# Grouped-query attention: three score blocks on VectorE in two jobs of three, and the checks and loads rearranged

## The chip, the core and the metric

The kernel runs on one core of a Trainium2 chip. The engines named here are TensorE (PE in the profile; PEld is its weight load), VectorE (DVE), ScalarE (ACT), GpSimd (POOL) and SyncE (SP, which here only issues DMAs). The metric is the device time of one execution in microseconds (us), as the median of several runs. Beside these, one execution was profiled; the trace and all durations come from that one.

## The reference

Grouped-query attention in float32: 8 batches, sequences of 512, 32 query heads, 8 key/value heads, head size 64. Four query heads share one key/value head.

```python
scale = 1.0 / np.sqrt(dim)
K_expanded = np.repeat(K, heads_per_group, axis=2)
V_expanded = np.repeat(V, heads_per_group, axis=2)
...
scores = np.einsum('bhqd,bhkd->bhqk', Q, K_expanded) * scale
weights = np.exp(scores - np.max(scores, axis=-1, keepdims=True))
weights = weights / (np.sum(weights, axis=-1, keepdims=True) + 1e-10)
output = np.einsum('bhqk,bhkd->bhqd', weights, V_expanded)
```

## The kernel before

**Jobs.** The work is cut into 64 jobs. Job j belongs to unit u = j // 2 and is one key/value head with its four query heads, in two pairs (i = 0, 1). Four units make a batch, so a batch is eight jobs. The scores of a job are 16 blocks of 128 keys x 512 queries: pair i, key chunk kc (four chunks of 128), head m within the pair. `scores` (L257) computes one block on TensorE with the keys as weights; the two heads of a pair lie in the two halves of the 128 rows.

**Exponentials.** Most blocks go through ScalarE: `act_tile` (L273) has TensorE write two blocks into a tile `s_ps` and ScalarE write their exponential into `pt` (L279). The pool of `s_ps` holds two tiles, so TensorE may be two tiles ahead. Some blocks of the second pair go through VectorE and GpSimd instead. `taken(j)` (L242) says how many: two in a narrow job, three in a wide one (`WIDE`, L41: every even job from 4 on). Their scores go to a tile `d_ps` (a pool of one tile with two banks of 512 columns), and then:

- `exp_d` (L283): VectorE turns them into 16-bit integers u (L290), two blocks in one instruction, the third block in one of its own;
- `exp_d2` (L297): VectorE takes the low bits f of u with an AND (L301), GpSimd computes g from f (L304) and w = g * f (L308);
- `exp_d4` (L314): VectorE adds u and w into `pt` (L317). This happens one job later; the text calls it the add.

In a wide job the fourth of seven ScalarE tiles, counted from 0, holds one block alone. It has no `s_ps` tile: its scores go into the second bank of the `d_ps` tile in whose first bank Q is transposed (L559 to L565), and ScalarE reads them there ("the half tile").

**Products.** `pv` (L333) multiplies the exponentials with V, to which a column of ones is appended, so that sums come out beside the products; 64 small matmuls a job, for the job before (`last`), in pieces between the score tiles (`cut`, L539, says where the second pair's are split). `norm` (L372) takes the reciprocal of the sums (L387) and multiplies into `o_sb` (L392) on VectorE. The pool of `pv` holds one tile, so the next 32 products wait for L392 of the 32 before. `store` writes a unit out through SP.

**Checks.** The exponentials need no maximum as long as sums stay within bounds and V is not huge. `check_sums` (L363) tests 16 pairs' reciprocals at a time with two VectorE operations (L356); `check_v` (L230) takes the largest absolute value of a quarter of a batch's V (L232). A slower general path runs behind a branch if a test fails; with these inputs it does not.

**Transposes and loads.** Q is loaded in its natural layout with a cast to bf16 (`load_q`, L132, GpSimd's queue), transposed by TensorE two jobs ahead (L210), and copied by VectorE into `qt` (L214). K is loaded the same way (`load_k`, L111) and transposed by DMA on SP's queue (`dma_k`, L185). V goes into one of two buffers (`load_v`, L120).

**Order.** The order of the program is the order in which each engine works: the code is issued under a manual schedule, nothing is rearranged, and every engine takes its instructions one after the other. The loop over jobs is L518 to L582. Where two instructions touch different banks of one tile, `apart` declares that they need not wait for each other; every other shared tile makes them wait. The third block of the next job is written into the second bank of the tile `bank` of this job, behind tile 5:

```python
act_tile(j, 5)
if taken(j + 1) > 2:
    exp_d(j + 1, 2, taken(j + 1), bank[:, 1:2, :], copies[0])()
pv(last, 1, *cut)
act_tile(j, 6)
pv(last, 1, cut[1], 32)
norm(last, 1)
```

Of the kernel before, what the change touches and what calls it, by code (L numbers as in the profile page):

```python
# [12 lines left out]
FP32 = mybir.dt.float32  # L13
BF16 = mybir.dt.bfloat16
# [4 lines left out]
ALU = mybir.AluOpType  # L19
EXP = mybir.ActivationFunctionType.Exp  # L20
COPY = mybir.ActivationFunctionType.Copy
AX = mybir.AxisListType
# [15 lines left out]
LAST_SUMS = NLAST * 2 * 4  # L38


WIDE = lambda j: j >= 4 and j % 2 == 0  # L41


@with_exitstack
# [23 lines left out]
def fast_path(ctx, tc, Q, K, V, out, flag, ident):  # L68
    nc = tc.nc
    B, S, H, D = Q.shape  # L70
    KV = K.shape[2]
    HPG = H // KV
    SC = S // 128
    GP = KV // 2
    NU = B * GP
# [6 lines left out]
    const_pool = ctx.enter_context(tc.tile_pool(name="const", bufs=1))  # L82
    qnat_pool = ctx.enter_context(tc.tile_pool(name="qnat", bufs=4))
# [11 lines left out]
    pv_pool = ctx.enter_context(tc.tile_pool(name="pv", bufs=1, space=PS))  # L95

    ok = const_pool.tile([128, SPB * 2 * SC], FP32, name="ok")
    okv = const_pool.tile([128, B * SC], FP32, name="okv")
    okall = const_pool.tile([128, 1], FP32, name="okall")
    gate = const_pool.tile([1, 1], FP16, name="gate")  # L100
    warm = const_pool.tile([128, S], BF16, name="warm")
# [2 lines left out]
    vt = [const_pool.tile([128, SC, KV, D + 1], BF16, name=f"v{j}") for j in range(2)]  # L104
# [4 lines left out]
    kn, qn, kt, qt, twice = {}, {}, {}, {}, {}  # L109

    def load_k(b, lo=0, hi=KV):  # L111
        if b not in kn:
            kn[b] = knat_pool.tile([128, SC, KV, D], BF16, name="k_nat")
        nc.gpsimd.dma_start(
            out=kn[b][:, :, lo:hi, :],
            in_=K[b, :, lo:hi, :].rearrange("(sc p) g d -> p sc g d", p=128),
        )


    def load_v(b, lo=0, hi=KV, chunks=range(SC)):  # L120
        for sc in chunks:
            nc.gpsimd.dma_start(  # L122
                out=vt[b % 2][:, sc, lo:hi, 0:D],
                in_=V[b, sc * 128:(sc + 1) * 128, lo:hi, :],
            )

    def load_v_head(b, g):
        nc.gpsimd.dma_start(
            out=vt[b % 2][:, :, g, 0:D], in_=V[b, :, g, :].rearrange("(sc p) d -> p sc d", p=128)
        )  # L130

    def load_q(u, lo=0, hi=2 * HPG):  # L132
        b, gp = divmod(u, GP)
        h0 = gp * 2 * HPG
        if u not in qn:
            qn[u] = qnat_pool.tile([128, SC, 2 * HPG, D], BF16, name="q_nat")
        nc.gpsimd.dma_start(  # L137
            out=qn[u][:, :, lo:hi, :],
            in_=Q[b, :, h0 + lo:h0 + hi, :].rearrange("(sc p) h d -> p sc h d", p=128),
        )  # L140

# [60 lines left out]
    def trans_q(j, bank, lo=0, hi=NPAIR, other=None):  # L202
        u, g = divmod(j, 2)
        ps = bank.bitcast(BF16).rearrange("p (i sc c) -> p i sc c", i=NPAIR, sc=SC)
        done = []
        for i in range(lo, hi):
            for sc in range(SC):
                h = g * HPG + 2 * i
                done.append(apart(
                    nc.tensor.transpose(ps[:, i, sc, :], qn[u][:, sc, h:h + 2, :], ident), other  # L210
                ))
        if u not in qt:
            qt[u] = qt_pool.tile([128, 2, NPAIR, S], BF16, name="qt")
        return done, lambda: apart(nc.vector.tensor_copy(  # L214
            out=qt[u][:, g, lo:hi, :], in_=ps[:, lo:hi, :, :].rearrange("p i sc c -> p i (sc c)")
        ), other)
# [10 lines left out]
                    apart(copy, before)  # L227
        pieces.append((bank, done, copy))

    def check_v(b, sc):  # L230
        n = b * SC + sc
        nc.vector.tensor_reduce(  # L232
            out=okv[:, n:n + 1], in_=vt[b % 2][:, sc, :, 0:D], op=ALU.max, axis=AX.XY,
            apply_absolute_value=True,
        )

    NJOB = NU * 2
    DPAIR = NPAIR - 1  # L240
# [1 line left out]
    def taken(j):  # L242
        return 1 if j == NJOB - 1 else 3 if WIDE(j) else 2

# [8 lines left out]
        return [[every[n] for n in group] for group in groups if group]  # L253

    jobs, osb, invs = {}, {}, {}

    def scores(j, ps, i, kc, m):  # L257
        u, g = divmod(j, 2)
# [38 lines left out]
    def exp_d2(j, engine=None):  # L297
        st = jobs[j]
        by_bits = engine is None
        engine = engine or nc.gpsimd  # L300
        nc.vector.tensor_single_scalar(  # L301
            out=st["f"], in_=st["u"], scalar=1023, op=ALU.bitwise_and
        )
        engine.tensor_scalar(  # L304
            out=st["g"], in0=st["f"], scalar1=-EXP_F1, scalar2=EXP_K * 2.0 ** (24 * by_bits),
            op0=ALU.add, op1=ALU.mult,
        )
        product = lambda: engine.tensor_tensor(  # L308
            out=st["w"], in0=st["g"], in1=st["f"].bitcast(FP16) if by_bits else st["f"],
            op=ALU.mult,  # L310
        )
        return product() if by_bits else product

    def exp_d4(j):  # L314
        st = jobs[j]
        n = taken(j)
        nc.vector.tensor_tensor(  # L317
            out=st["pt"][:, DPAIR, :, :, :].rearrange("p kc m q -> p (kc m) q")[
                :, d_block(j):d_block(j) + n, :
            ].bitcast(U16),  # L320
            in0=st["u"],
            in1=st["w"],
            op=ALU.add,
        )
# [38 lines left out]
    def check_sums():  # L363
        while full:
            k, n = full.pop()
            cols = n * 2 * SC
            flat = invs.pop(k).rearrange("p s m qc -> p (s m qc)")[:, 0:cols]
            in_bounds((ok[:, 0:cols], ok[:, 0:cols]), flat, ok[:, 0:cols])
# [79 lines left out]
        return s_pool.tile([128, 2, S], FP32, name="s_ps")  # L448

    def key_head(g, queue):  # L450
        queue.dma_start(out=kf[g], in_=K[0, :, g, :].rearrange("(sc p) d -> p sc d", p=128))

    key_head(0, nc.sync)
    nc.scalar.dma_start(out=qf, in_=Q[0, :, 0:2, :].rearrange("(sc p) h d -> p sc h d", p=128))
# [5 lines left out]
    for j in range(2):  # L460
        nc.gpsimd.memset(vt[j][:, :, :, D:D + 1], 1.0)
    load_k(0, 2, 4)
    load_q(1)
    load_v_head(0, 1)
    load_k(0, 4, KV)
    load_v(0, 2, KV)
    nc.gpsimd.memset(ones, 1.0)
    nc.gpsimd.memset(ok, 1.0)

# [48 lines left out]
    for j in range(1, NJOB - 1):  # L518
        last = j - 1
        u, g = divmod(j, 2)  # L520
        b, gp = divmod(u, GP)
        open_job(j)
        if j == 1:

            nc.gpsimd.tensor_copy(out=gate, in_=jobs[0]["pt"][0:1, 0, SC - 1, 0, 0:1])
            load_q(2)
            load_q(3)
        if g == 0 and u >= 1 and u + 3 < NU:
            load_q(u + 3)
        if (gp, g) == (1, 0) and b + 1 < B:  # L530
            load_k(b + 1)
        if 3 <= 2 * gp + g < 3 + SC and b + 1 < B:
            load_v(b + 1, chunks=(2 * gp + g - 3,))
        if j == 1:
            dma_k(0, 2)
        if gp == 2 and g == 0 and b + 1 < B:
            dma_k(b + 1)

        cut = (4, 18) if taken(j) > 2 else (11, 19)  # L539
        act_tile(j, 0)  # L540
        if j == 1:
            piece(1, *first_k(1, 0, bank[:, 1, S // 2:]))
        exp_d(j, 0, 2, d_tile())()
        act_tile(j, 1)

        if j == 8:
            check_v(0, 0)
        if g == 1 and 1 < j and b < B - 1:
            check_v(b, gp)
        if 0 <= j - 8 * (B - 1) < SC:  # L550
            check_v(B - 1, j - 8 * (B - 1))
        pv(last, 0, 0, 16)
        act_tile(j, 2)
        pv(last, 0, 16, 32)
        norm(last, 0)
        act_tile(j, 3)

        reads = []
        bank = d_tile()  # L559
        beside = act_tile(j, 4, bank) if taken(j) > 2 else None  # L560

        ahead = (j + 1,) if j < 2 else (3, 4) if j == 2 else (j + 2,)
        for n, to in enumerate(ahead):
            if to < NJOB:
                reads.append(trans_q(to, bank[:, n, :], other=beside)[1])  # L565
        if j == 1:
            reads.append(first_k(1, 1, bank[:, 1, :])[1])
        exp_d4(last)
        check_sums()
        exp_d2(j)  # L570
        copies = [read() for read in reads]
        if taken(j) == 2:
            act_tile(j, 4)
        pv(last, 1, 0, cut[0])
# [7 lines that stand above are left out]
        del jobs[last]  # L582
# [146 lines left out]
```

## Time and profile before

| | |
|---|---|
| median of 3 runs | 411.63 us (411.63 to 411.84) |
| the profiled execution | 412.08 us |
| its span, first to last instruction | 410.3 us |
| busy: ScalarE | 401.0 us (98% of the span), 454 instructions |
| busy: TensorE | 377.9 us (92%) |
| busy: VectorE | 342.3 us (83%) |
| busy: GpSimd | 305.9 us (75%) |
| waiting longest: GpSimd's g for VectorE's f | 90.9 us in 62 waits |
| granted TensorE clock | 0.999 |

How to read the lines below. A timeline line gives the start, the duration, the engine, the line of the kernel, the operation, and what it writes and reads; "x16" merges 16 like instructions in a row, and then the duration runs from the first start to the last end. A line of groups gives the number of instructions behind the x, then their busy time in us and the mean duration of one in ns, and behind the next bar the idle time of the engine just ahead of them and what ended it. A line of waits reads: who waited for whom, us in total, how many times, the longest. Instructions of one engine overlap: one starts while the one before it drains, so durations add up to more than the busy time. In the stretch that is used most, the job that starts at 198.99 us is narrow (j = 31) and the one that starts at 205.41 us is wide (j = 32).

### The profile page before, as it was taken

How to read it: one execution, taken by the hardware profiler on the slowest of the kernel's cores; microseconds unless marked ns; L12 is line 12 of the kernel's file. 1: busy time of each engine (PE TensorE's matmuls, PEld its weight loads, DVE VectorE, ACT ScalarE, POOL GpSimd, SP SyncE). 2: the span in 40 equal slices, each digit the busy share in tenths (PEclk: the TensorE clock that was granted, in tenths of full speed). 3: DMA queues.
4: the chain of work that ended last, by engine and by line, in shares of the span. 5: the costliest groups of instructions: out<-in, count | busy, mean ns of one | idle time of the engine just before them, and what ended most of it. 6: DMA issues, size and time to landing. Idle time of an engine off the chain costs nothing.

```text
span 410.3 us, 13045 instructions
## 1 busy us (share of the span) xinstructions
PE 377.9 (92%) x5666; PEld 233.0 (57%) x5666; DVE 342.3 (83%) x608; ACT 401.0 (98%) x454; POOL 305.9 (75%) x216
## 2 busy tenths in 40 slices
PE   7999999999999999999999999999999999999985
PEld 3565565555555655655555655655655555655543
DVE  4787898888898888888888888888889888998775
ACT  5999999999999999999999999999999999999995
POOL 9858767888678777688777897587786887676562
PEclk9999999999999999999999999999999999999999
DMA  9999974999839995499995999669996799752206
GB/s 142 167 242 166 201 158 138 188 148 214 170 109 227 126 263 127 113 211 107 203 255 83 205 188 215 157 84 215 183 191 155 132 205 204 145 144 104 104 18 195
DMA packets 93278, 67.74 MB, mean 165 GB/s; under 512 B 53280, under 2 KB 76320, under 8 KB 93216
## 3 DMA queue, kind: packets, MB, share of 16 engines
q0 software_dynamic: 55488, 24.91, 54.6%
q1 hardware_dynamic: 36672, 41.56, 36.6%
q8 instruction: 45, 0.74, 0.8%
q10 hardware_dynamic: 1056, 0.39, 0.4%
q14 instruction: 17, 0.14, 0.1%
HBM read 50.33 MB, written 33.55 MB: 204 GB/s over the span
## 4 chain that ended last, share of the span: by engine, by line
ACT 88%; PE 8%; DVE 2%; issue 1%; ACTq 0%; DVEq 0%
ACT pt L279 88%; PE s_ps L261 5%; PE pv L345 2%; PE s_ps L473 1%; DVE o_sb L392 1%; DVE pt L317 0%; ACTq L279 0%; DVE inv_last L387 0%; DVE qt L214 0%; PE pv L490 0%; PE d_ps L345 0%; DVE u L290 0%; ACT qt L495 0%; PE d_ps L261 0%; DVE ok L356 0%
## 5 line engine op out<-in xcount | busy, mean ns | idle before, releaser
L279 ACT ACTIVATE pt<-s_ps 128x1024 f16<-128x1024 f32 x419 | 396.3, 1295 | 0.7 <-PE s_ps L261 0.7
L345 PEld LDWEIGHTS <-pt 128*128 128x128 f16 x4096 | 142.3, 98 | 75.7 <-issue 55.3
L345 PE MATMUL pv<-v,pt 128*128 128x65 bf16 x4064 | 179.4, 195 | 0.9 <-DVE o_sb L392 0.7
L261 PE MATMUL s_ps<-qt,kt 64*128 64x512 bf16 x781 | 153.3, 383 | 23.3 <-ACT pt L279 17.1
L308 POOL TENSOR_TENSOR w<-g,f 128x1024 bf16<-128x1024 bf16 (+1 forms) x63 | 162.9, 2586 | 5.2
L304 POOL TENSOR_SCALAR g<-f 128x1024 bf16<-128x1024 int16 (+1 forms) x63 | 78.3, 1242 | 91.0 <-DVE f L301 90.9
L290 DVE TENSOR_SCALAR u<-d_ps 128x1024 int16<-128x1024 f32 (+1 forms) x94 | 97.6, 1038 | 0.5 <-PE d_ps L261 0.5
L261 PEld LDWEIGHTS <-kt 64*128 64x128 bf16 x960 | 55.3, 93 | 66.2 <-issue 37.0
L392 DVE TENSOR_TENSOR o_sb<-pv,inv 128x512 f32<-128x512 f32 x121 | 83.7, 692 | 4.2
L387 DVE RECIPROCAL inv<-pv 128x8 f32<-128x8 f32 x121 | 25.1, 207 | 49.7 <-PE pv L345 49.7
L317 DVE TENSOR_TENSOR pt<-u,w 128x1536 uint16<-128x1536 int16 (+1 forms) x64 | 51.4, 803 | 0.3 <-POOL w L308 0.2
L261 PE MATMUL d_ps<-qt,kt 64*128 64x512 bf16 x179 | 46.1, 375 | 0.1
L214 DVE COPY qt<-d_ps 128x1024 bf16<-128x1024 bf16 x62 | 42.3, 683 | 0.0
L210 PEld LDWEIGHTS <-q_nat 128*128 128x128 bf16 x508 | 28.5, 98 | 20.2 <-issue 20.2
L210 PE MATMUL d_ps<-ident,q_nat 128*128 128x128 bf16 x496 | 38.3, 221 | 0.0
L301 DVE TENSOR_SCALAR f<-u 128x1536 int16<-128x1536 int16 (+1 forms) x64 | 30.7, 480 | 0.0
L122 POOL DMA_DIRECT2D v<-in_V_dram x32 | 29.0, 914 | 0.0
L137 POOL DMA_DIRECT2D q_nat<-in_Q_dram x33 | 27.0, 820 | 0.1
L279 ACT ACTIVATE pt<-d_ps 128x512 f16<-128x512 f32 x30 | 26.7, 889 | 0.0
L232 DVE TENSOR_REDUCE okv<-v 128x1 f32<-128x512 bf16 x32 | 21.6, 675 | 0.0
L261 PE MATMUL s_ps<-qt,kt_first 64*128 64x512 bf16 x56 | 11.2, 390 | 2.1 <-ACT pt L279 1.7
L261 PEld LDWEIGHTS <-kt_first 64*128 64x128 bf16 x64 | 4.1, 93 | 6.0 <-issue 3.5
(54 smaller groups left out, 46.8 us busy)
## 6 DMA issues: line engine op xcount, KB each, us to landing
out_dram<-o_sb SPq DMA_DIRECT2D x31, 1024.0 KB, 7.2
q_nat<-in_Q_dram POOLq DMA_DIRECT2D x31, 512.0 KB, 6.1
k_nat<-in_K_dram POOLq DMA_DIRECT2D x7, 512.0 KB, 8.7
v<-in_V_dram POOLq DMA_DIRECT2D x28, 128.0 KB, 7.2
kt<-kt SPq DMA_DIRECT2D x14, 256.0 KB, 4.1
out_dram<-o_sb SPq DMA_DIRECT2D x4, 256.0 KB, 2.2
kt<-k_nat SPq DMA_TRANSPOSE x32, 5.9
v<-in_V_dram POOLq DMA_DIRECT2D x4, 96.0 KB, 8.3
```

Of the source, the lines that this page charges most:

```text
L122: nc.gpsimd.dma_start(out=vt[b % 2][:, sc, lo:hi, 0:D], in_=V[b, sc * 128:(sc + 1) * 128, lo:hi, :],)
L210: nc.tensor.transpose(ps[:, i, sc, :], qn[u][:, sc, h:h + 2, :], ident), other
L214: return done, lambda: apart(nc.vector.tensor_copy(out=qt[u][:, g, lo:hi, :], in_=ps[:, lo:hi, :, :].rearrange("p i sc c -> p i (sc c)")), ...
L261: return nc.tensor.matmul(ps, keys[64 * m:64 * m + 64, g if u == 0 else g ^ m, kc * 128:(kc + 1) * 128], qt[u][64 * m:64 * m + 64, g, i, : ...
L279: return nc.scalar.activation(out=jobs[j]["pt"][:, i, kc, lo:, :], in_=ps[:, lo:, :], func=EXP, scale=scale)
L290: return lambda: nc.vector.tensor_scalar(out=st["u"][:, lo:hi, :], in0=ps[:, 0:hi - lo, :], scalar1=A_U, scalar2=B_U, op0=ALU.mult, op1=AL ...
L301: nc.vector.tensor_single_scalar(out=st["f"], in_=st["u"], scalar=1023, op=ALU.bitwise_and)
L304: engine.tensor_scalar(out=st["g"], in0=st["f"], scalar1=-EXP_F1, scalar2=EXP_K * 2.0 ** (24 * by_bits), op0=ALU.add, op1=ALU.mult,)
L308: product = lambda: engine.tensor_tensor(out=st["w"], in0=st["g"], in1=st["f"].bitcast(FP16) if by_bits else st["f"], op=ALU.mult,)
L317: nc.vector.tensor_tensor(out=st["pt"][:, DPAIR, :, :, :].rearrange("p kc m q -> p (kc m) q")[:, d_block(j):d_block(j) + n, :].bitcast(U16 ...
L345: nc.tensor.matmul(st["pv"][i][:, m, qc, :], st["pt"][:, i, kc, m, qc * 128:(qc + 1) * 128], vt[b % 2][:, kc, 2 * gp + g, :], start=(n < 2 ...
L392: nc.vector.tensor_tensor(out=osb[u][:, :, h:h + 2, :].rearrange("p qc m d -> p m qc d"), in0=sums[:, :, :, 0:D], in1=inv[:, :, :, None].t ...
```

## The change

- **Wide jobs.** From job 4 on, two jobs of every three take three blocks on VectorE (j = 4, 5, 7, 8, ..., 61, 62) instead of every second one. The first wide job after a narrow one is called W1 below, the second W2. `cut` gets a third form for W2.
- **Order on VectorE.** `exp_d2(j)` (the AND, and with it GpSimd's g and w) stands ahead of `exp_d4(last)` (the add). `check_sums` stands behind the copies of Q and runs in narrow jobs only.
- **Checks of V.** One check covers half a batch's V instead of a quarter. The two of a batch stand in its first two narrow jobs (from j = 3 on), behind the copies, instead of ahead of the products.
- **Loads.** `load_q` loads the eight heads of two units at once, into tiles twice as large; V of a batch comes in one DMA; all loads of the loop follow a table. K and V take row 4p + sc where they took row 128 sc + p, which changes the order of the keys in both alike.

```diff
-WIDE = lambda j: j >= 4 and j % 2 == 0
+WIDE = lambda j: j >= 4 and j % 3 > 0
...
-            in_=K[b, :, lo:hi, :].rearrange("(sc p) g d -> p sc g d", p=128),
+            in_=K[b, :, lo:hi, :].rearrange("(p sc) g d -> p sc g d", p=128),
...
+    def load_v(b, lo=0):
+        to = vt[b % 2][:, :, lo:, 0:D]
+        of = V[b, :, lo:, :].rearrange("(p sc) g d -> p sc g d", p=128)
+        if lo:
+            for sc in range(SC):
+                nc.gpsimd.dma_start(out=to[:, sc], in_=of[:, sc])
+        else:
             nc.gpsimd.dma_start(
-                out=vt[b % 2][:, sc, lo:hi, 0:D],
-                in_=V[b, sc * 128:(sc + 1) * 128, lo:hi, :],
+                out=to.rearrange("p sc g d -> p (sc g) d"),
+                in_=of.rearrange("p sc g d -> p (sc g) d"),
             )
...
-            qn[u] = qnat_pool.tile([128, SC, 2 * HPG, D], BF16, name="q_nat")
+            qn[p] = qnat_pool.tile([128, SC, 4 * HPG, D], BF16, name="q_nat")
...
-    def check_v(b, sc):
-        n = b * SC + sc
+    def check_v(b, half):
+        n = 2 * b + half
         nc.vector.tensor_reduce(
-            out=okv[:, n:n + 1], in_=vt[b % 2][:, sc, :, 0:D], op=ALU.max, axis=AX.XY,
-            apply_absolute_value=True,
-        )
+            out=okv[:, n:n + 1], in_=vt[b % 2][:, 2 * half:2 * half + 2, :, 0:D], op=ALU.max,
+            axis=AX.XYZ, apply_absolute_value=True,
+        )
...
+    CHECKS = {}
+    for b in range(B):
+        rest = [j for j in range(max(3, 8 * b + 1), 8 * b + 8) if not WIDE(j)]
+        CHECKS.update(zip(rest, [(b, half) for half in range(2)]))
+
+    LOADS = {
+        1: ((load_q, 1, 0, 8), (load_q, 1, 8, 16)), 2: ((load_q, 2),),
+        3: ((load_k, 1), (load_v, 1)), 4: ((load_q, 3), (load_q, 4)), 7: ((load_k, 2), (load_q, 5)),
+        10: ((load_v, 2),), 13: ((load_q, 6),), 16: ((load_k, 3), (load_q, 7)), 19: ((load_v, 3),),
+        22: ((load_k, 4), (load_q, 8)), 25: ((load_q, 9),), 28: ((load_v, 4),),
+        31: ((load_k, 5), (load_q, 10)), 34: ((load_v, 5),), 37: ((load_q, 11), (load_q, 12)),
+        40: ((load_k, 6), (load_q, 13)), 43: ((load_v, 6),), 46: ((load_q, 14), (load_q, 15)),
+        49: ((load_k, 7),), 52: ((load_v, 7),),
+    }
...
-        cut = (4, 18) if taken(j) > 2 else (11, 19)
+        cut = (11, 19) if taken(j) < 3 else (4, 18) if taken(last) < 3 else (4, 16)
...
-        if j == 8:
-            check_v(0, 0)
-        if g == 1 and 1 < j and b < B - 1:
-            check_v(b, gp)
-        if 0 <= j - 8 * (B - 1) < SC:
-            check_v(B - 1, j - 8 * (B - 1))
...
+        exp_d2(j)
         exp_d4(last)
-        check_sums()
-        exp_d2(j)
         copies = [read() for read in reads]
+        if not WIDE(j):
+            check_sums()
+        if j in CHECKS:
+            check_v(*CHECKS[j])
```

More of the change, by code (lines that the diff above doesn't have):

```diff
@@ L97, in fast_path @@
     ok = const_pool.tile([128, SPB * 2 * SC], FP32, name="ok")
-    okv = const_pool.tile([128, B * SC], FP32, name="okv")
+    okv = const_pool.tile([128, B * 2], FP32, name="okv")
     okall = const_pool.tile([128, 1], FP32, name="okall")
@@ L115, in load_k @@
             out=kn[b][:, :, lo:hi, :],
-            in_=K[b, :, lo:hi, :].rearrange("(sc p) g d -> p sc g d", p=128),
+            in_=K[b, :, lo:hi, :].rearrange("(p sc) g d -> p sc g d", p=128),
         )
-    def load_v(b, lo=0, hi=KV, chunks=range(SC)):
-        for sc in chunks:
+    def load_v(b, lo=0):
[5 more added lines that the diff above has]
+        else:
             nc.gpsimd.dma_start(
-                out=vt[b % 2][:, sc, lo:hi, 0:D],
-                in_=V[b, sc * 128:(sc + 1) * 128, lo:hi, :],
+                out=to.rearrange("p sc g d -> p (sc g) d"),
+                in_=of.rearrange("p sc g d -> p (sc g) d"),
             )
@@ L128, in load_v_head, with load_q @@
         nc.gpsimd.dma_start(
-            out=vt[b % 2][:, :, g, 0:D], in_=V[b, :, g, :].rearrange("(sc p) d -> p sc d", p=128)
+            out=vt[b % 2][:, :, g, 0:D], in_=V[b, :, g, :].rearrange("(p sc) d -> p sc d", p=128)
         )
[L132 to L135, printed above, removed]
-            qn[u] = qnat_pool.tile([128, SC, 2 * HPG, D], BF16, name="q_nat")
+    def load_q(p, lo=0, hi=4 * HPG):
+        b, at = divmod(p, GP // 2)
+        h0 = at * 4 * HPG
+        if p not in qn:
+            qn[p] = qnat_pool.tile([128, SC, 4 * HPG, D], BF16, name="q_nat")
         nc.gpsimd.dma_start(
-            out=qn[u][:, :, lo:hi, :],
+            out=qn[p][:, :, lo:hi, :],
             in_=Q[b, :, h0 + lo:h0 + hi, :].rearrange("(sc p) h d -> p sc h d", p=128),
@@ L207, in trans_q @@
             for sc in range(SC):
-                h = g * HPG + 2 * i
+                h = (u % 2) * 2 * HPG + g * HPG + 2 * i
                 done.append(apart(
-                    nc.tensor.transpose(ps[:, i, sc, :], qn[u][:, sc, h:h + 2, :], ident), other
+                    nc.tensor.transpose(ps[:, i, sc, :], qn[u // 2][:, sc, h:h + 2, :], ident),
+                    other,
                 ))
@@ L450, in key_head @@
     def key_head(g, queue):
-        queue.dma_start(out=kf[g], in_=K[0, :, g, :].rearrange("(sc p) d -> p sc d", p=128))
+        queue.dma_start(out=kf[g], in_=K[0, :, g, :].rearrange("(p sc) d -> p sc d", p=128))
     key_head(0, nc.sync)
@@ L462, in fast_path @@
     load_k(0, 2, 4)
-    load_q(1)
+    load_q(0, 8, 16)
     load_v_head(0, 1)
     load_k(0, 4, KV)
-    load_v(0, 2, KV)
+    load_v(0, 2)
     nc.gpsimd.memset(ones, 1.0)
@@ L525, in fast_path @@
             nc.gpsimd.tensor_copy(out=gate, in_=jobs[0]["pt"][0:1, 0, SC - 1, 0, 0:1])
[L526 to L533, printed above, removed]
+        for load, *of in LOADS.get(j, ()):
+            load(*of)
         if j == 1:
```

## The prediction

> **What bounds the kernel now.** I read the page's chain first, then the groups by form, then one narrow and one wide job in the timeline, engine by engine. The chain that ended last is ScalarE nearly all the way:
>
> ```profile
> ACT 88%; PE 8%; DVE 2%; issue 1%; ACTq 0%; DVEq 0%
> L279 ACT ACTIVATE pt<-s_ps 128x1024 f16<-128x1024 f32 x418 | 395.8, 1296 | 0.7 <-PE s_ps L261 0.7
> L279 ACT ACTIVATE pt<-d_ps 128x512 f16<-128x512 f32 x30 | 26.7, 889 | 0.0
> PE s_ps L261 <- ACT pt L279: 18.8, 65, 0.5
> ```
>
> ScalarE sat idle 0.7 us for its exponentials in the whole run. A mean of 1296 ns is not what one costs, since they overlap; the spacing of their ends is. In the timeline of a wide job (it starts at 205.41, when TensorE writes its first scores):
>
> ```profile
> 207.71 2.23 ACT L279 ACTIVATE pt<-s_ps 128x1024 f16<-128x1024 f32 x2
> 209.52 0.91 ACT L279 ACTIVATE pt<-d_ps 128x512 f16<-128x512 f32 x1
> 210.00 3.18 ACT L279 ACTIVATE pt<-s_ps 128x1024 f16<-128x1024 f32 x3
> ```
>
> Ends fall at 209.94, 210.43 and 213.18, the last being three tiles on: 0.917 us for a full tile, 0.49 for the half tile. A job takes 6.42 us narrow and 5.99 wide. How late may TensorE be? A tile that ScalarE meets with an empty queue takes 1.02 us (the one at 394.14, whose scores started at 393.70), so from the start of the scores to the end of the exponential 1.45 us pass. Scores may thus start 1.45 us ahead of the tile's end on ScalarE's grid, about 0.33 us later than most now start. Anything beyond is lost for good.
>
> **Edit 1, two wide jobs of three.** Wide jobs become 40 instead of 30. Each drops half a tile: 0.917 - 0.49 = 0.427; ten give **-4.27 us**. That is all the change can gain on this chain.
>
> But now a wide job (W1) is followed by a wide one (W2), which before never occurred. L577 then puts the next job's third block into the second bank of the tile in which ScalarE reads this job's half tile (L560). TensorE has, in the wide job of before:
>
> ```profile
> 209.26 0.30 PE L345 MATMUL pv<-v,pt 128*128 128x65 bf16 x4
> 209.49 0.39 PE L261 MATMUL s_ps<-qt,kt 64*128 64x512 bf16 x2
> 209.82 0.61 PE L345 MATMUL pv<-v,pt 128*128 128x65 bf16 x14
> 210.36 0.39 PE L261 MATMUL s_ps<-qt,kt 64*128 64x512 bf16 x2
> ```
>
> The third block stands right behind the pair of 209.49 and must wait for the half tile's end at 210.43; a score pair that waits for ScalarE starts 0.05 after it (212.31 after 212.26). So 210.48; 0.31 until the products behind it start (203.79 to 204.09 in a narrow job, whose third block waits for nobody); 14 products and the switch 0.54 (209.82 to 210.36); tile 6's scores at 211.33, its exponential ends at 212.78. The grid had 212.26: 0.52 us lost. Queued behind the waiting matmul are those 14 products and tile 6, for which ScalarE waits. W1 occurs 20 times (j = 4, 7, ..., 61): **+10.4 us**. Bounds: 0.40 if the 0.31 is only the 0.21 from pair to single, 0.60 if the next job's first tile (57 ns of room left) slips too.
>
> **Edit 2, the check of V.** A reduce of 128x512 takes 675 ns (32 times) and now stands where VectorE idles 0.27 us before the reciprocal. After: 16 reduces of 128x1024, in narrow jobs, behind the copy of Q. That shape is in no row; between 0.675 and 1.35, I take 1.21, since u takes 680 ns on 512 columns and 1214 on 1024. VectorE in a narrow job of before:
>
> ```profile
> 201.84 0.21 DVE L387 RECIPROCAL inv<-pv 128x8 f32<-128x8 f32 x1 [0.27 <-PE pv L345]
> 202.09 0.69 DVE L392 TENSOR_TENSOR o_sb<-pv,inv 128x512 f32<-128x512 f32 x1
> 202.69 0.95 DVE L317 TENSOR_TENSOR pt<-u,w 128x1536 uint16<-128x1536 int16 x1
> 203.56 0.42 DVE L301 TENSOR_SCALAR f<-u 128x1024 int16<-128x1024 int16 x1
> 203.89 0.69 DVE L214 COPY qt<-d_ps 128x1024 bf16<-128x1024 bf16 x1
> 204.50 0.68 DVE L290 TENSOR_SCALAR u<-d_ps 128x512 int16<-128x512 f32 x1
> ```
>
> The check takes the place at 204.50 (each starts 0.08 before the end of the one ahead). Then u starts at 205.62, the reciprocal at 206.22, o_sb ends at 207.16 instead of 206.35. The next job's products, due at 206.65, wait for o_sb until 207.22; 16 of them and the switch take 0.60, so tile 2's scores start at 207.82. Their limit is 209.02 - 1.45 = 207.57: 0.25 lost.
>
> **Edit 3, the order AND, add.** By itself 0: copies start when they did. The checks of the sums (two L356 operations, 0.53 us together at 67.09) move behind the copies, and run only in narrow jobs. All seven full ones fall into a narrow job that also checks V (j = 9, 18, 27, 33, 42, 51, 57).
>
> What is new is who runs beside whom. Before, AND, add and sum checks run between the end of w and the start of g, with GpSimd computing nothing (its 90.9 us of waiting for f). After, AND releases g while add runs, and the sum checks meet g and w. No row shows add beside g; neighbours do:
>
> ```profile
> 5.51 0.78 POOL L128 DMA_DIRECT2D v<-in_V_dram  x1
> 5.83 0.57 DVE L167 CAST twice<-kf 128x256 bf16<-128x256 f32 x1
> 10.17 0.43 DVE L301 TENSOR_SCALAR f<-u 128x1024 int16<-128x1024 int16 x1
> 10.22 0.40 POOL L467 MEMSET ones<- 128x1 bf16 x1
> L424 POOL TENSOR_SCALAR right<-inv_last,okall x3: 383/430/714, 403.5 to 406.1; 128x40 bf16<-128x40 f32 x2, 128x16 bf16<-128x16 f32 x1
> ```
>
> The cast ends 0.11 us after GpSimd's instruction (its twin at 4.15 took 0.34); a one-column memset beside AND takes 403 ns and ends 0.03 after it (others of one column 98 to 115); the L424 operation that lies beside a VectorE product of two SBUF tiles takes 714 ns, its twin 430, 0.28 more. Against it: the twin cast also had a load beside it, and 13 adds beside a load took 948 ns, 17 alone 949. So the cost of a meeting lies between nothing and the rest of the other's instruction. I take the latter, the value that three of these rows are nearest to.
>
> Worked out, with the times of the wide job above: in W2, AND 209.26 (0.14 late from W1's wait), add to 210.68, only then g (1.47) and w (3.09), to 215.35: 3.95 us into the narrow job, that is 202.94 there. AND, ready at 202.69, starts at 202.99, 0.30 late. In a narrow job with a V check alone, u then ends at 206.61, the next job's first VectorE block starts on TensorE at 206.67 and tile 1's scores at 206.89 (limit 208.10 - 1.45 = 206.65: 0.24 lost); o_sb ends at 207.46, tile 2 starts at 208.12 (limit 207.81 by now: 0.31). Together 0.55, nine times: **+4.9 us**.
>
> With sum checks: add ends 204.28, g holds until 205.33; the first check, ready at 204.80, runs to 205.62; w, waiting since 205.42, comes next and holds 2.12 us to 207.74; the second check ends at 208.03, the V check at 209.16, u at 209.76. Tile 1's scores start at 210.04: 3.39 lost, and o_sb (210.61) costs tile 2 another 0.31. 3.70, seven times: **+25.9 us**.
>
> The Trainium skill (SBUF — State Buffer, Who interferes with whom) says that VectorE and GpSimd share one pair of SBUF ports, held for a whole instruction, and that a VectorE operation with two SBUF inputs contends with a GpSimd one that reads SBUF. The trace agrees in the 714 against 430 ns, but shows no GpSimd product holding up VectorE. By that rule the sum is 449.0, without it 425.8.
>
> **Edit 4, the loads.** Same bytes; Q issues halve, V goes from four issues a batch (914 ns each for 1024 pieces of one head) to one of 4096 pieces. Bounds 0.91 and 3.66 us; the 765 ns of the two 512-piece loads put it near 1.8. Loads stand at the start of W1, where GpSimd is free from 2.2 to 4.3 us into the job: covered, cost 0. If 3.66 holds, AND and g wait 1.5 us six times, at most +9. Data lands in 6 to 9 us and is due two jobs or more later; only K of batch 1 (j = 3, transposed from j = 4) makes SP wait, some 5 us, with one store behind it that three o_sb buffers cover.
>
> **Sum,** against the profiled execution (412.08; span 410.3): -4.27 + 10.4 + 4.9 + 25.9 = +36.9, 449.0. The median shown is 0.45 below the profiled one: **448.6 us**.
>
> **Rivals.** (a) Meetings cost nothing: nine times 0.25 and seven times 0.77 (0.53 more on VectorE: 0.46 at tile 1, 0.31 at tile 2) are 7.6: 425.8, median 425.4. For it: the 948 against 949. (b) They cost, but the second sum check starts ahead of w: 1.61 instead of 3.70, 434.0. It needs VectorE to win by 0.03 us over an instruction already waiting. (c) VectorE's lateness is hidden, only W1 costs: 417.8. Against it: room is 0.33, o_sb is late by 0.8. (d) Faster: the third block's wait stays within TensorE's room. It decides at 210.81 (212.26 - 1.45) for tile 6's scores; I find 211.33. With the checks hidden too, 407.4.
>
> **Chances.** Forecast 0.42, (b) 0.15, (a) 0.25, (c) 0.07, (d) and other gains 0.04, no change 0.01, above 452 (loads, more meetings) 0.06. The range 424 to 452 takes in forecast, (b) and (a), 0.82. Within 0.2% is about what a measurement cannot tell from no change. Faster 0.04, same 0.01, slower 0.95.
>
> **What would show it.** In each W1, d_ps L261 waiting about 0.77 us for ACT pt, and one gap of 1.43 instead of 0.917 between ScalarE's ends; if absent, the 10.4 is wrong. V checks of 1.2 us. Narrow jobs with sum checks: the second L356 starting after w's end, and 3 to 4 us idle on ScalarE in the next job; if the two still take 0.6 us together, (a) or (b) holds. g starting at add's end, not 0.1 after AND's. A V issue on GpSimd above 2.1 us would add to it.

## The result, and the profile after

The changed kernel takes 456.11 us (median of 6 runs, 451.59 to 469.62) where the kernel before takes 411.84 on the same chip: 1.103 times the time, 95% interval 1.099 to 1.107. The ratio leaves out runs more than 1.5% above their kernel's fastest; the median of the four that stay is 453.9. The profiled execution took 453.28 us (span 451.5), 41.2 more than the profiled one of before. The prediction said 448.6, at most 452: the direction was right, the time was above the range.

First the page's chain and the groups by form, in the columns used before:

```profile
PE 46%; DVE 22%; ACT 19%; DMA 7%; issue 2%; SPq 1%; POOL 1%; ACTq 0%
```

```profile
L298 ACT ACTIVATE pt<-s_ps 128x1024 f16<-128x1024 f32 x408 | 386.3, 1094 | 40.4 <-PE s_ps L280 39.3
L323 POOL TENSOR_SCALAR g<-f 128x1024 bf16<-128x1024 int16 x23 | 37.2, 1618 | 11.8 <-DVE f L320 11.7
L238 DVE TENSOR_REDUCE okv<-v 128x1 f32<-128x1024 bf16 x16 | 19.3, 1206 | 0.0
L375 DVE SCALAR_TENSOR_TENSOR ok<-inv,ok 128x128 f32<-128x128 f32 x14 | 18.9, 1349 | 0.2
```

ScalarE's share of the chain fell from 88% to 19%: its exponentials now wait 39.3 us for scores where they waited 0.7. That is nearly the whole difference, so the account can be made on ScalarE: every gap beyond the normal spacing (0.917 us for a full tile, 0.49 for a half) is lost time. Two of the other lines stand out. The 14 sum checks have a mean of 1349 ns (288 before), and g on 1024 columns takes 1618 ns (1039 before). These are the lines of before:

```profile
L304 POOL TENSOR_SCALAR g<-f 128x1024 bf16<-128x1024 int16 x33 | 34.3, 1039 | 40.9 <-DVE f L301 40.8
L356 DVE SCALAR_TENSOR_TENSOR ok<-inv,ok 128x128 f32<-128x128 f32 x14 | 4.0, 288 | 0.2
```

The waits after say who was late:

```profile
PE d_ps L280 <- DVE u L309: 27.5, 17, 3.2
PE d_ps L280 <- ACT pt L298: 5.6, 15, 0.6
PE s_ps L280 <- DMA kt<-kt: 3.8, 1, 3.8
```

ScalarE waits for TensorE (the 39.3 us above); TensorE in turn waits for VectorE's u (up to 3.2 us), for ScalarE's half tile (0.6 at most) and once, 3.8 us, for the transposed K. These are three different causes, and each has its place in the timeline.

**W1's third block.** TensorE and then ScalarE in job 16, a wide job with a wide one behind it:

```profile
120.95 0.39 PE L280 MATMUL s_ps<-qt,kt 64*128 64x512 bf16 x2
121.94 0.37 PE L280 MATMUL d_ps<-qt,kt 64*128 64x512 bf16 x1 [0.59 <-ACT pt L298]
122.24 0.61 PE L364 MATMUL pv<-v,pt 128*128 128x65 bf16 x14
122.78 0.39 PE L280 MATMUL s_ps<-qt,kt 64*128 64x512 bf16 x2
...
121.05 0.83 ACT L298 ACTIVATE pt<-d_ps 128x512 f16<-128x512 f32 x1
121.53 1.27 ACT L298 ACTIVATE pt<-s_ps 128x1024 f16<-128x1024 f32 x1
123.21 1.02 ACT L298 ACTIVATE pt<-s_ps 128x1024 f16<-128x1024 f32 x1 [0.41 <-PE s_ps L280]
```

The half tile ends at 121.88 (121.05 + 0.83), and the third block starts 0.06 later. The 14 products start 0.30 behind that, tile 6's scores 0.54 behind them. On ScalarE, tile 5 ends at 122.80 and tile 6 at 124.23: 1.43 us, as forecast, instead of 0.917.

**A narrow job with sum checks.** VectorE and then GpSimd in job 18:

```profile
133.08 0.42 DVE L320 TENSOR_SCALAR f<-u 128x1024 int16<-128x1024 int16 x1
133.42 0.95 DVE L336 TENSOR_TENSOR pt<-u,w 128x1536 uint16<-128x1536 int16 x1
134.28 0.68 DVE L220 COPY qt<-d_ps 128x1024 bf16<-128x1024 bf16 x1
134.89 2.73 DVE L375 SCALAR_TENSOR_TENSOR ok<-inv,ok 128x128 f32<-128x128 f32 x2
137.54 1.20 DVE L238 TENSOR_REDUCE okv<-v 128x1 f32<-128x1024 bf16 x1
138.67 0.67 DVE L309 TENSOR_SCALAR u<-d_ps 128x512 int16<-128x512 f32 x1
...
130.02 3.09 POOL L327 TENSOR_TENSOR w<-g,f 128x1536 bf16<-128x1536 bf16 x1
133.59 1.68 POOL L323 TENSOR_SCALAR g<-f 128x1024 bf16<-128x1024 int16 x1 [0.47 <-DVE f L320]
135.35 2.12 POOL L327 TENSOR_TENSOR w<-g,f 128x1024 bf16<-128x1024 bf16 x1
```

g, released by AND at 133.50, ends 0.90 after the add's end, nearly as if it had begun there (alone it takes 1.04). The first sum check is over 0.14 after g's end; the second, which starts 0.09 behind the start of w, takes 2.17 us and ends at 137.62, 0.15 after w. The V check and u come behind it, and u frees the bank for the next job's first block only at 139.34. What follows on TensorE stands in this table by stage; the columns are window, length, busy time and count of PE, PEld, DVE, ACT and POOL, the granted clock, DMA share and GB/s:

```profile
136.40:139.50 3.10, 0.10 (x2) 0.10 (x3) 3.07 (x5) 1.16 (x2) 2.77 (x2) 1.00 0.00 0
139.50:142.90 3.40, 3.17 (x41) 1.68 (x38) 2.21 (x4) 2.05 (x2) 0.00 (x0) 0.69 1.79 115
```

TensorE is idle for 3.0 of 3.1 us. The 0.69 behind that is a mean: the granted clock stays full until 140.8 and is then 0.50 for 3.4 us, until 144.2. The 16 products of 141.37 take 1.06 us where they take 0.66 elsewhere.

**K of batch 1.** SP's queue in jobs 4 to 6 before, the same after, then TensorE at the start of job 8:

```profile
31.07 5.76 SPq L188 DMA_TRANSPOSE kt<-k_nat  x4
42.44 1.11 SPq L193 DMA_DIRECT2D kt<-kt  x2
...
34.67 12.95 SPq L193 DMA_TRANSPOSE kt<-k_nat  x4
52.16 1.11 SPq L198 DMA_DIRECT2D kt<-kt  x2
...
61.32 0.61 PE L280 MATMUL s_ps<-qt,kt 64*128 64x512 bf16 x1 [3.82 <-DMA kt<-kt]
```

These lines time the issuing on the queue, not the data; the copies (`kt<-kt`) are issued once the last transpose has landed. Before, that was 11.4 us behind the first transpose, now it is 17.5. The copies then landed at 47.27 before (4.8 us) and land at 61.27 now (9.1 us). So K comes 14.0 us later: 3.6 because it is loaded a job later, 6.1 in the transposes and 4.3 in the copies. Job 8 needs it at 57.5 and waits.

The account of the profiled execution, from ScalarE's gaps:

| | predicted, us | measured, us |
|---|---|---|
| ten more half tiles | -4.27 | -4.27 |
| W1's third block, 20 times | +10.4 | +10.3 (0.51 each) |
| V check alone | +4.9 (9 x 0.55) | +1.85 (8 x 0.23; job 3's costs nothing) |
| sum checks with V check, 7 times | +25.9 (3.70 each) | +28.0 (3.7 to 4.2 each) |
| loads: K of batch 1 in job 8 | 0 | +5.5 (4.40, 0.52 and 0.60 at three tiles) |
| sum | +36.9 | +41.4; +41.2 between the two executions |

### The profile page after: what moved, and what is told of

The parts are those of the page before. It is cut to its first block, busy times and chain, and to the rows that moved or that the text cites. A ratio compares the mean times of both kernels' runs of the same rounds, so it can differ in the third digit from the quotient of the medians.

```text
span 451.5 us, 12936 instructions
## 1 busy us (share of the span) xinstructions
PE 390.4 (86%) x5666; PEld 233.0 (52%) x5666; DVE 365.7 (81%) x602; ACT 402.7 (89%) x454; POOL 328.1 (73%) x181
## 4 chain that ended last, share of the span: by engine, by line
PE 46%; DVE 22%; ACT 19%; DMA 7%; issue 2%; SPq 1%; POOL 1%; ACTq 0%
PE pv L364 24%; ACT pt L298 18%; PE s_ps L280 17%; DVE o_sb L411 6%; DVE ok L375 4%; DVE okv L238 4%; PE d_ps L280 3%; DVE pt L336 3%; PE d_ps L215 3%; DMA kt<-k_nat 3%; DVE u L309 2%; DMA kt<-kt 2%; DMA k_nat<-in_K_dram 2%; DVE inv L406 1%; DVE f L320 1%
## 5 line engine op out<-in xcount | busy, mean ns | idle before, releaser
L298 ACT ACTIVATE pt<-s_ps 128x1024 f16<-128x1024 f32 x409 | 386.8, 1093 | 40.4 <-PE s_ps L280 39.3
L323 POOL TENSOR_SCALAR g<-f 128x1536 bf16<-128x1536 int16 (+1 forms) x63 | 116.0, 1842 | 110.1 <-DVE f L320 110.0
L327 POOL TENSOR_TENSOR w<-g,f 128x1536 bf16<-128x1536 bf16 (+1 forms) x63 | 172.6, 2739 | 5.3
L309 DVE TENSOR_SCALAR u<-d_ps 128x1024 int16<-128x1024 f32 (+1 forms) x104 | 104.4, 1003 | 4.8 <-PE d_ps L280 4.7
L280 PEld LDWEIGHTS <-kt 64*128 64x128 bf16 x960 | 49.5, 94 | 82.1 <-issue 53.2
L280 PE MATMUL d_ps<-qt,kt 64*128 64x512 bf16 x199 | 55.6, 388 | 33.4 <-DVE u L309 27.5
L375 DVE SCALAR_TENSOR_TENSOR ok<-inv,ok 128x128 f32<-128x128 f32 (+1 forms) x16 | 19.3, 1209 | 0.3
L238 DVE TENSOR_REDUCE okv<-v 128x1 f32<-128x1024 bf16 x16 | 19.3, 1206 | 0.0
L142 POOL DMA_DIRECT2D q_nat<-in_Q_dram x19 | 15.0, 792 | 0.1
L127 POOL DMA_DIRECT2D v<-in_V_dram x7 | 12.3, 1750 | 0.0
```

Of the source, the lines that this page charges most:

```text
L238: nc.vector.tensor_reduce(out=okv[:, n:n + 1], in_=vt[b % 2][:, 2 * half:2 * half + 2, :, 0:D], op=ALU.max, axis=AX.XYZ, apply_absolute_va ...
L280: return nc.tensor.matmul(ps, keys[64 * m:64 * m + 64, g if u == 0 else g ^ m, kc * 128:(kc + 1) * 128], qt[u][64 * m:64 * m + 64, g, i, : ...
L298: return nc.scalar.activation(out=jobs[j]["pt"][:, i, kc, lo:, :], in_=ps[:, lo:, :], func=EXP, scale=scale)
L309: return lambda: nc.vector.tensor_scalar(out=st["u"][:, lo:hi, :], in0=ps[:, 0:hi - lo, :], scalar1=A_U, scalar2=B_U, op0=ALU.mult, op1=AL ...
L323: engine.tensor_scalar(out=st["g"], in0=st["f"], scalar1=-EXP_F1, scalar2=EXP_K * 2.0 ** (24 * by_bits), op0=ALU.add, op1=ALU.mult,)
L327: product = lambda: engine.tensor_tensor(out=st["w"], in0=st["g"], in1=st["f"].bitcast(FP16) if by_bits else st["f"], op=ALU.mult,)
```

## The experiments

The theory behind the account: three independent stalls of TensorE (W1's bank, the sum checks that wait for a whole GpSimd instruction, K late in job 8) and a small one (V). The rivals: VectorE is merely overloaded or in the wrong order; the loads' stall is an effect of the other stalls; wide jobs of this number cannot pay at all. Each run was made beside runs of the kernel before, which had a median of 411.72 to 411.88. The first four take one cause out of the changed kernel.

**Sum checks by one-input reduces.** The smallest and the largest of the reciprocals are kept, and the bounds tested once at the end.

```diff
-            in_bounds((ok[:, 0:cols], ok[:, 0:cols]), flat, ok[:, 0:cols])
+            for row, op in enumerate((ALU.min, ALU.max)):
+                nc.vector.tensor_reduce(out=ends[:, row, k:k + 1], in_=flat, op=op, axis=AX.X)
```

> The changed kernel, but the sums are checked by two reduces (least and largest reciprocal of the 16 pairs) in place of the two L375 operations, at the same place, on the same data; bounds are tested at the end. A reduce has one SBUF input, the L375 operation two. Theory (the two-input operations wait for GpSimd's g and w): the two take about 0.3 us each without waiting, the seven jobs lose about 0.7 us instead of 4.0, so 23 us go: about 430 us in the profiled execution (453.3 now). Rival 1 (VectorE is simply full or late there, whatever stands in the place): within 3 us of 453. Rival 2 (GpSimd holds up any VectorE operation on SBUF): the reduces wait as long, 450 to 456.

Measured: 438.47 us (425.69 to 444.64, 4 runs; too far apart for an interval), profiled 444.64. The group of these reduces, and one job's pair in the timeline, beside a g of 145.23 to 146.91:

```profile
L383 DVE TENSOR_REDUCE ends<-inv 128x1 f32<-128x128 f32 x14 | 3.3, 273 | 0.0
```

```profile
146.53 0.47 DVE L383 TENSOR_REDUCE ends<-inv 128x1 f32<-128x128 f32 x2
```

Two instructions on the same data at the same place, but with one SBUF input each, run beside g without waiting: 273 ns instead of 1349. The seven jobs lose 0.61 to 0.73 instead of about 4, and behind the sum checks the clock stays up. So it was neither the order nor VectorE's load, but the operation with two SBUF inputs. That a reduce also writes less (one column, not 128) does not explain it: the products into `o_sb`, with one input in SBUF and one in PSUM, write 512 columns, and the 72 that run beside g or w in the changed kernel keep their 690 to 693 ns. One SBUF input is no general protection, though, as the last run below shows. The total missed, because K was later still in this execution: jobs 4 and 8 lost 6.5 and 13.0 us to it. Without these 19.5 it is 425.1, against 424.5 for the expected 430 without after's 5.5.

**K of batch 1 loaded one job earlier.**

```diff
-        1: ((load_q, 1, 0, 8), (load_q, 1, 8, 16)), 2: ((load_q, 2),),
-        3: ((load_k, 1), (load_v, 1)), 4: ((load_q, 3), (load_q, 4)), 7: ((load_k, 2), (load_q, 5)),
+        1: ((load_q, 1, 0, 8), (load_q, 1, 8, 16)), 2: ((load_k, 1), (load_q, 2)),
+        3: ((load_v, 1),), 4: ((load_q, 3), (load_q, 4)), 7: ((load_k, 2), (load_q, 5)),
```

> The changed kernel, but K of batch 1 is loaded in job 2, ahead of Q, as before the change, instead of in job 3. Theory (its late transposes hold up job 8's first tile once): the gap of 4 us at the start of job 8 and the one of 0.5 to 0.6 in the tiles behind it go: 5 to 5.5 us less, 448 us profiled, and the runs spread less. Rival (the fewer, larger loads are late in general): the wait moves to another job or stays, 452 to 454.

Measured: 449.88 us (449.47 to 455.84, 4 runs), ratio 1.097 (1.089 to 1.105), profiled 449.47. Job 8 loses nothing and nobody waits for K, though its copies are still issued 17.3 us behind the first transpose (27.25 to 44.57): all of it starts 7.4 us earlier. The other losses are as in the changed kernel (3.7 to 4.3 in the jobs with sum checks).

**The third block behind the 14 products** in wide jobs, so that it asks for its bank later.

```diff
+        if taken(j) > 2:
+            pv(last, 1, *cut)
         if taken(j + 1) > 2:
             exp_d(j + 1, 2, taken(j + 1), bank[:, 1:2, :], copies[0])()
-        pv(last, 1, *cut)
+        if taken(j) == 2:
+            pv(last, 1, *cut)
```

> The changed kernel, but in wide jobs the next job's third block stands behind the 14 products instead of ahead of them. Theory (TensorE idles until ScalarE has read the half tile, with the products queued behind): the 0.51 us at tile 6 of each first wide job goes, 20 times: 10 us less, 443 us profiled. Rival (the wait moves to VectorE: the third block's u comes 0.2 us later, then the reciprocal and o_sb, and the next job's products wait): less than 4 us less, 449 to 453.

Measured: 448.29 us (447.21 to 458.95, 5 runs), ratio 1.087 (1.086 to 1.089). The profiled execution was the slowest, 458.95, with K late by 14.5 us in job 8 and 1.4 in job 4. W1's 0.51 is gone from the thirteen W1 without sum checks: 0.0, or up to 0.08 behind a V check. The seven with sum checks lose 31.4 us in all, against 31.9 in the changed kernel, so there nothing was gained: behind three of these stalls, instead of one, the clock stayed at 0.50 for 6.8 us. Without K this execution is 442.0, 5.8 less than the changed kernel without K (447.8), where the theory had 10 and the rival less than 4.

**V checked by quarters at the old place**, ahead of the products.

```diff
+        if j == 8:
+            check_v(0, 0)
+        if g == 1 and 1 < j and b < B - 1:
+            check_v(b, gp)
+        if 0 <= j - 8 * (B - 1) < SC:
+            check_v(B - 1, j - 8 * (B - 1))
...
-        if j in CHECKS:
-            check_v(*CHECKS[j])
```

> The changed kernel, but V is checked by quarters of a batch, ahead of the products, as before the change; all else as changed. Theory (the check of 1.2 us behind the copies makes the third block's u and o_sb late): 0.23 us in eight jobs goes, and 1.1 us in each of the seven jobs that also check sums: about 9.5 us less, 444 us profiled. Rival (VectorE's time is only shifted, the quarter checks delay the reciprocal in wide jobs instead): 450 to 456.

Measured: 441.38 us (437.94 to 452.37, 4 runs), ratio 1.072 (1.068 to 1.075), profiled 437.94. The 0.23 of the V jobs is gone. The jobs with sum checks lose 1.8 to 3.6 instead of about 4. So the V check costs more behind the sum checks than alone, because it lengthens the one stall that has no room left. K was late by only 0.8 here; without the 4.7 that this saves, the execution gained 10.6, near the 9.5 expected.

**All four together.**

> The changed kernel with four places mended at once: sums checked by two reduces, K of batch 1 loaded in job 2, the third block behind the 14 products in wide jobs, V checked by quarters ahead of the products. Theory (these four places hold the whole loss): what is left is the 4.27 us that ten more wide jobs save, about 408 us profiled and 407.5 median. Rival (the order of AND and add, or the larger loads, cost by themselves): above 411.

Measured: 408.80 us (407.96 to 435.63, 4 runs), ratio 0.993 (0.991 to 0.995), profiled 407.96: -4.1 beside the -4.27 of the half tiles. Left over are 0.10 in job 2 and 0.49 in job 62. The three causes and the small one are all there is in this execution. The run of 435.63 had no profile, and it had K early: its cause stays open.

The next four add one part of the change to the kernel before. **The wide jobs alone:**

```diff
-WIDE = lambda j: j >= 4 and j % 2 == 0
+WIDE = lambda j: j >= 4 and j % 3 > 0
...
-        cut = (4, 18) if taken(j) > 2 else (11, 19)
+        cut = (11, 19) if taken(j) < 3 else (4, 18) if taken(last) < 3 else (4, 16)
```

> The kernel before with two wide jobs of three and the third form of the cut, nothing else. Theory: ten half tiles saved (-4.27) and 0.51 us lost in each of 20 first wide jobs (+10.3): 418.1 us profiled, 417.7 median. Rival (the third block's wait is hidden when VectorE has its old order): 407.5. Rival (VectorE cannot carry three blocks in two jobs of three): above 425.

Measured: 417.98 us (417.87 to 418.35, 4 runs), ratio 1.015 (1.013 to 1.017), profiled 418.35: 0.50 to 0.52 at tile 6 in each of the 20 W1, and nothing else.

**The order alone**, with sum checks in narrow jobs, V untouched:

```diff
-        exp_d4(last)
-        check_sums()
         exp_d2(j)
+        exp_d4(last)
         copies = [read() for read in reads]
+        if not WIDE(j):
+            check_sums()
```

> The kernel before with the new order on VectorE alone: AND ahead of the add, the sum checks behind the copies and in narrow jobs only; wide jobs, V checks and loads as before. Theory (sum checks meet GpSimd's g and w, and TensorE's clock falls behind the stall): the second L356 operation takes over 2 us, seven jobs lose 1.8 to 3.5 us each, 425 to 436 us. Rival (the order is harmless, the loss needs the V check in the same job): 411 to 413.

Measured: 430.37 us (430.31 to 431.64, 4 runs), ratio 1.046 (1.044 to 1.048), profiled 430.31. The sum checks have the same mean as in the changed kernel, 1349 ns, and seven jobs lose 1.8 to 3.1. That the order is harmless without the V check falls: the new order with the sum checks' new place costs 18 us by itself.

**The loads alone** (load_k, load_v, load_q and the table as in the change; V checked as before):

> The changed kernel's loads (Q for two units, V for a batch, K of batch 1 in job 3, new order of the keys) with everything else as before. Theory: no cost but the late K of batch 1, which holds up job 8 once (0.8 to 14 us in the runs so far): 412 to 424 us, and runs that differ by several us where the kernel before stays within 0.3. Rival (the late K was the stalls' doing): 411 to 412.

Measured: 428.72, 421.65, 415.13 and 428.77 us (median 425.19, no interval). In the profiled execution (428.72), the only losses are 4.6 in job 4, for the second half of batch 0's K, and 12.3 in job 8, for batch 1's. The copies of batch 1 were issued at 64.59, 29.5 us behind the first transpose. None of the other stalls is there, so the rival, that these made K late, falls. It is a cost of the loads, and it varies: 3 to 17 us in these four runs.

**What delays K:** the same, with the two Q loads of job 4 (1 MB each) moved to jobs 6 and 9, K where it is.

```diff
-        4: ((load_q, 3), (load_q, 4)),
+        6: ((load_q, 3),), 9: ((load_q, 4),),
```

> The kernel of e10 (the changed loads alone), but the two 1 MB loads of Q that stand in job 4, right ahead of the transposes of K of batch 1 on SP, are moved to jobs 6 and 9; K stays in job 3. Theory A (the four transposes share the DMA engines with 2 MB of Q, 13 to 14 us instead of 5.8): the transposes take about 6 to 8 us again and job 8 has no gap; what is left is a gap at job 4 in some runs, 412 to 417 us. Theory B (K in job 3 is itself too late, whatever else is loaded): the gap at job 8 stays, 415 to 429 us.

Measured: 411.94 us (411.56 to 421.23, 10 runs), ratio 1.000 (0.998 to 1.001). SP's queue of this kernel:

```profile
34.57 5.96 SPq L193 DMA_TRANSPOSE kt<-k_nat  x4
43.56 1.11 SPq L198 DMA_DIRECT2D kt<-kt  x2
```

The transposes start when they did in the changed kernel, but the copies are issued 9.0 us behind the first instead of 17.5, and the loads cost nothing. So K's later issue alone does no harm, and the 2 MB of Q beside it do none where K comes a job earlier, as above: the loss takes both. The gap in job 4 is another matter: batch 0's K was transposed at 14 us, ahead of these two loads. It is absent here, but absent in the changed kernel's profile too, so its cause stays open. One run of ten, 421.23, has no profile: some rest of the load table may still do it, as perhaps in the runs of 435.63 and 455.84 above.

Three runs asked what wide jobs can give. **Wide jobs as in the change and the third block late, all else as before** (the edits of the wide jobs alone and of the late third block):

> The kernel before with two wide jobs of three, the third form of the cut, and the third block behind the 14 products in wide jobs. Theory: only the saving is left, -4.27 us: 407.8 us profiled, 407.4 median, faster than both kernels. Rival (VectorE, with the old order, becomes late in the second wide job): 409 to 415.

Measured: 408.72 us (408.53 to 408.95, 4 runs), ratio 0.992 (0.991 to 0.994), profiled 408.95. That is 3.1 of the 4.27; the rest goes in small steps, half of it in jobs 62 and 63.

**All jobs from 4 on wide, third block late, order as before** (`WIDE = lambda j: j >= 4`):

> The kernel before with every job from 4 to 62 wide, the third block behind the 14 products, and the cut (4, 16) behind a wide job; order, checks and loads as before. ScalarE alone would save 29 half tiles: 12.4 us, 399.7 us profiled. But add, AND, g and w of consecutive wide jobs form a loop: 0.87 + 0.47 + 0.10 + 1.47 + 0.08 + 3.09 = 6.08 us against the 5.99 of a wide job. Theory: the loop bounds it, 0.1 us in each of 58 jobs: 404 to 407 us profiled. Rival (VectorE or GpSimd cannot carry it, loads on GpSimd come on top): above 411.

Measured: 423.22 us (423.16 to 423.32, 4 runs), ratio 1.028 (1.026 to 1.030): a miss by 16. Its waits:

```profile
PE d_ps L261 <- DVE u L290: 22.7, 55, 0.7
```

TensorE waits for VectorE in almost every job, and ScalarE loses 0.5 to 0.8 in the even jobs and 0.2 in the odd ones. In an odd job VectorE does the V check and `o_sb`, then waits for w with the add (0.59 in job 15), and is late with u and the next `o_sb` behind it. Whether the V check is the cause was not tested.

**The same in the mended kernel**, where AND goes ahead of the add (the kernel of all four mends, all jobs wide, sum checks in any job):

> The mended kernel (AND ahead of the add, sums by two reduces, K early, V by quarters, third block behind the products) with every job from 4 to 62 wide. With AND first, g waits for the end of the add that runs beside it, so the loop is no shorter: w to AND or add 0.1, AND 0.47, add 0.87, g 1.47, w 3.09. Theory: 6.0 to 6.1 us a job, 403 to 407 us profiled, within 2 us of the same with the old order. Rival (g does not wait for the add): 400.

Measured: 407.52 us (407.08 to 407.81, 4 runs), ratio 0.990 (0.988 to 0.991): the fastest of all, faster than both kernels. That the old order would do as well within 2 us falls: 423.22 against 407.52, with the loads and the reduces as further differences between the two. AND first gives GpSimd its work earlier, which may be the reason; how much of the 15.7 is the order alone was not run. And AND first has a price here: eleven times it started while w was still running, and each time it ended 0.42 us behind w, the slowest after 1049 ns instead of 550, though it has one SBUF input only.

## Why the prediction was right, and where it was wrong

**Half tiles and W1** (Edit 1): right in mechanism and size. The wide jobs alone gave 418.35 profiled; the forecast's two terms make 418.2. Rivals (c) and (d) fall: (c) because VectorE's lateness was not hidden, (d) because the wait is beyond TensorE's room, as 1.43 us between two ends shows. The idle time in front of the third block is 0.59, not the 0.77 named ahead: idle time counts from the end of the pair, 209.88 in the lines of before, and from there to 210.48 it is 0.60.

**V check** (Edit 2): the reduce took 1206 ns (1.21 estimated) and alone costs 0.23 (0.25 worked out). The mis-sized term is the 0.30 by which AND was to be held by w: w of W2 ended 3.76 us into the narrow job (at 133.12), not 3.95, only 0.03 after AND had started, and AND kept its normal 417 ns. That w can hold AND is right: with all jobs wide it did, as the last run shows. So +1.85, not +4.9.

**Sum checks** (Edit 3): the mechanism was right in every step named ahead: g at the add's end, the second check behind w, V check and u behind that. (In the record g starts 0.09 behind AND's end; that it waited for the add shows in its end.) Rivals (a) and (b) fall with the 1349 ns. The size, 28.0 against 25.9, is off both ways: tile 1 loses 2.6 to 3.0 instead of 3.39, but tile 2 loses 0.5 to 0.9 instead of 0.31, and tile 3 another 0.6 where nothing was forecast. Tiles 2 and 3 fall into the stretch with the granted clock at 0.50, which the forecast did not have. The weighing that mattered was that of rows: three neighbours pointed to a wait for a whole instruction, and a fourth (adds beside a load) to none. The Trainium skill (SBUF — State Buffer, Who interferes with whom) gave the same answer, and the 273 ns of the one-input reduce beside g agrees with its condition of two SBUF inputs.

**Loads** (Edit 4): this is the step that failed: "Data lands in 6 to 9 us and is due two jobs or more later; only K of batch 1 ... makes SP wait, some 5 us, with one store behind it that three o_sb buffers cover." I followed what stands behind K on SP, and not K itself. The durations were those of loads that ran with little beside them; 2 MB of Q then ran beside the transposes: the copies behind them were issued 17.5 us after the first transpose, not 11.4, and took 9.1 us to land, not 4.8. With the start a job later K came 14.0 us later, and the copies that landed at 61.27 were due at 57.5. The term put at 0 is 5.5 us in the profiled execution, which is more than the whole difference between 449.0 and 453.3: with 2.1 more in the sum checks, 3.05 less in V, and some 0.3 less in small terms, the forecast comes to 453.2. With K a job earlier and all else as changed, the median was 449.88, inside the range. The other executions of the changed kernel lie between 451.59 and 469.62. That K comes earlier or later in them was not seen, as they have no profile; but the runs of the loads alone differ by 13.6 us, and the four experiments with the loads of before by 1.3 at most (the kernel before itself once took 416.44). My 0.06 for "above 452 (loads, more meetings)" was too low for a resource whose time under load no row had shown.

## What to carry to other kernels

When a change lets two engines work at once that took turns before, look first at whether they can: an instruction with one input in place of one with two may make the whole difference (273 against 1349 ns here), but read it from a row, since AND with its one input did wait (1049 against 550). A load that lands in time beside little may not do so beside megabytes: follow each moved load through to the first instruction that needs its data, with the transfers that now run beside it. And write into a shared bank only when its reader is done: moving one matmul behind 14 products turned 1.015 into 0.992.

## What the runs showed of the hardware

- A TensorE stall costs more than its length. Around or just behind each of the seven idle stretches of 3.2 us in the changed kernel the granted clock was 0.50 for 3.4 us, once for 6.8; a score pair then ran 0.61 us instead of 0.39, 16 products 1.06 instead of 0.66. With 14 idle stretches of 2.1 to 2.4 us (order alone, V by quarters) it did so ten times, with seven of 0.9 to 1.05 us (sum checks by reduces) never. The Trainium skill (TensorE: Matmul & The Clock Gate, Part 1) has the clock throttled after about 3.4 us of idling; the traces agree in kind, but here 3.2 us sufficed every time, and 2.1 us mostly.
- A VectorE operation with two SBUF inputs and a GpSimd one hold each other up in both directions: the sum check took 2176 ns behind w (288 before), and g took 1618 ns behind the add (1039 before). Whichever started first was served first: the first check started behind g and ended 0.14 us behind it, and the second started 0.09 behind w and ended 0.15 behind it.
- With one SBUF input it depends on the operation: reduces ran beside g undisturbed (273 ns), while AND, started during w, ended 0.42 us behind w's end in eleven cases of eleven (all jobs wide, AND first).
- The copies behind the four transposes of batch 1's K were issued 9.0 to 12.3 us after the first transpose, but 16 to 31 us after it beside 2 MB of Q loads. In job 8, K was late by 0.8 to 14.5 us between kernels with these same loads, for which no run here gives a reason.
